# Operand tiles in slots of 4608 bytes with other row starts, in one step of a hybrid decoder on one core

## The chip, the cores and the metric

The kernel runs on one core of a Trainium2 chip. The metric is the device time of one execution in microseconds. Three runs of the kernel before took 1588.73, 1588.81 and 1589.09 us, a median of 1588.81.

## What is computed

One inference step of one decoder layer over 264 tokens: 8 sample tokens and a prompt of 256, each of 2048 features. The reference, cut to its order:

```python
proj = rmsnorm(x) @ w_in                       # 2048 x 6144: u_A, v_A, q, k, v, g
out_a = gelu(u) * chunk_spatial_mix(layernorm(gelu(v_A)))
out_b = silu(g) * groupnorm(retention(rotary(q), rotary(k), v, state))
h = x + concat(out_a, out_b) @ w_out           # 2048 x 2048
mk, mv = rmsnorm(mem) @ w_ck, rmsnorm(mem) @ w_cv      # 256 memory tokens
h = h + cross_attend(rmsnorm(h) @ w_cq, mk, mv) @ w_co # samples: cached keys, values
h = h + square(relu(rmsnorm(h) @ w_ff1)) @ w_ff2       # 2048 x 8192 x 2048
y = rmsnorm(h)
```

All data is float32. Outputs beside y are the memory's keys and values, the retention states and the normed rows of the sample tokens.

## The kernel before

Activations lie transposed: a feature block of 128 on the partitions, the 264 tokens along the free dimension. A tile of weights ("chunk" in the code) is 2 feature blocks of 128 by 512 output columns. Its float32 numbers are split into a rounded part and the rest, `wh` (cast by ScalarE, line 1064) and `wl` (subtracted by VectorE, line 1072). The activations are split in the same way into `xh` and `xl`, or under the names `h1`, `h2`, `mg`, `mu`, `o`, `q` and `r` with h and l behind. `group_act` (lines 156 to 158) issues per weight tile, for each of 4 column blocks m and each of the 2 feature blocks k, three matmuls: `wh` by `xh`, `wh` by `xl`, `wl` by `xh`. The weights stand still in the array and a row of activations, 264 numbers or 1056 bytes a partition, moves past them. That is 6 matmuls for each m and 24 for each tile.

Tiles of 264 columns: 12 column groups by 8 tiles of the input projection, 4 by 8 each of `w_out`, `w_cq` and `w_co`, 16 by 8 of `w_ff1` and 8 by 4 by 4 of `w_ff2`, whose very last group goes through `group_last` with the m outermost. The two projections of the memory tokens have operands of their own (`memh`, `meml`: rows of 256 numbers). `w_ck` goes through `group_act` with n=256, `w_cv` through `group_mem`, where the weights move.

A pair of operand tiles comes from `rows` (line 50): each holds four feature blocks, so `opnd_of` takes block kt from row kt % 4 of tile kt // 4, and the weight tiles of a group go through the rows 0, 1, then 2, 3, then 0, 1 of the next operand tile, and so on. `rows` takes one of 26 slots under the tag "s", which `slot` hands out for other things too. A slot is as large as its largest tile: here 4 rows by 272 numbers by 4 bytes, 4352 bytes, 17 times 256. In the built program the first slot begins at byte 72128 of a partition, which is 192 behind a multiple of 256. The rows are 1088 bytes apart, so the four rows of every tile begin 192, 0, 64 and 128 bytes behind a multiple of 256.

The order of the work is written out by hand. A loop over all 512 weight tiles issues the casts two or three tiles ahead, the loads up to six ahead (all on SP's queue), and the matmuls. After every 6 matmuls (fewer in some groups) `run_point` lets one deferred piece of other work go ahead: evictions, rotary, retention by head in two lanes, sample attention, stores. A store goes out ten such points after it was asked for. Retention of a head (line 601) copies the new prompt state out of PSUM into `so` (line 640), asks for its store, then scales the old state (line 642) and updates it by rows. Sample attention multiplies each loaded tile of cached keys or values with a broadcast query or probability on VectorE (lines 854 and 877). The sums are what is wanted; the products go to a scratch tile `jk` of the tag "hf".

Of the kernel before, what the change touches and what calls it, by code (L numbers as in the profile page):

```python
# [6 lines left out]
F32 = mybir.dt.float32  # L7
F32R = mybir.dt.float32r
AF = mybir.ActivationFunctionType
ALU = mybir.AluOpType  # L10
# [32 lines left out]
def _emit(tc, cst, wpool, spool, tpool, psum, dpool, I, O):  # L43
# [4 lines left out]
        return spool.tile(shape, dt, name=name, tag="s", bufs=NSLOT)  # L48

    def rows(name):  # L50
        return spool.tile([128, 4, 272], F32R, name=name, tag="s", bufs=NSLOT)

    def t264(name="t"):
        return tpool.tile([128, T], F32, name=name, tag="t", bufs=9)
# [5 lines left out]
        return tpool.tile([128, n], F32, name=name, tag="sm", bufs=24)  # L60

    def half(name, dt=F32):
        return tpool.tile([128, 512], dt, name=name, tag="hf", bufs=3)

    def bank(shape, name):
        return psum.tile(shape, F32, name=name, tag="mm", bufs=5)
# [228 lines left out]
            S[key] = r  # L295

    def opnd_of(tiles):
        return lambda kt: (tiles[kt // 4][0][:, kt % 4, 0:T], tiles[kt // 4][1][:, kt % 4, 0:T])

    def opnd_mem(kt):  # L300
        return tuple(t[:, kt % 4, :] for t in memop[kt // 4])
# [26 lines left out]

    def prep_x(s, ks=R4):
        for k in ks:  # L330
            split(A[s][0][:, k, 0:T], A[s][1][:, k, 0:T], hT[s][:, k, :], gain(G_N1, 4 * s + k))

    def square_x():
        q = []
# [73 lines left out]
    def ev_vA(g):  # L408
        def ev(ps):
            z = normed(ps)  # L410
            ge = slot([128, 4, T], "ge")
            if g == 0:
                sgu_loads()
                S["vn"] = [slot([128, 1024], "vn0"), slot([128, 1024], "vn1"), slot([8, 1024], "vns")]
                S["vsum"] = [small(2, "vsum") for _ in range(3)]

            def natural():
                for i, (c0, n) in enumerate(TOK):
                    tp = misc([n, 512], "tp")
                    for m in R4:  # L420
                        transpose(tp[:, m * 128:(m + 1) * 128], ge[:, m, c0:c0 + n])
                    act.activation(S["vn"][i][:, g * 512:(g + 1) * 512], tp[:], AF.Copy, scale=0.5,
                                   accum_out=S["vsum"][i][0:n, g:g + 1])
                    yield

            def gen():
                yield from gelu2(z, lambda m: ge[:, m, :])
                defer(natural(), 1)
                if g == 0:
                    chain(masks(), 12)  # L430
                else:
                    chain(layernorm(), 12)
                    for h in range(8):
                        defer(spatial(h), 56)
            chain(gen())
        return ev
# [26 lines left out]
    def masks():  # L463
        gp.tensor_tensor(out=S["wst"][:], in0=S["wst"][:], in1=trilt.unsqueeze(1).broadcast_to([128, 8, 128]),
                         op=ALU.mult)
        dg = cst.tile([8, 8, 8], F32, name="dg")
        gp.tensor_tensor(out=dg[:], in0=ident[0:8, 0:8].unsqueeze(1).broadcast_to([8, 8, 8]),
                         in1=w00[:].unsqueeze(2).broadcast_to([8, 8, 8]), op=ALU.mult)
        S["dg"] = dg
        yield  # L470
        S["spat"] = [slot([128, 4, T], "spat") for _ in range(2)]
# [19 lines left out]

    def split4(dst, src):
        for m in R4:
            act.copy(dst[0][:, m, 0:T], src[m][:])
        yield
        for m in R4:
            dve.tensor_tensor(out=dst[1][:, m, 0:T], in0=src[m][:], in1=dst[0][:, m, 0:T].bitcast(F32),
                              op=ALU.subtract)

    def pair(name):  # L500
# [76 lines left out]
    def sample_rows(g):  # L577
        if g == 0:
            S["kqd"], S["kqe"] = {}, {}
        cols = S["rpool"].tile([128, 2, 32], F32, name="kqcol", tag="kqcol", bufs=1)  # L580
        for i, w in enumerate("kq"):
            act.copy(cols[:, i, :].rearrange("p (m b) -> p m b", m=4), S[w][g][:, :, 0:8])
        yield 2
        tp = misc([32, 2, 128], "tp")
        for i in range(2):
            transpose(tp[:, i, :], cols[:, i, :])
        rows = half("kqrow")[0:32, 0:256]
        act.copy(rows, tp[:].rearrange("p a d -> p (a d)"))
        S["kqd"][g] = dpool.tile([32, 256], F32, name=f"kqd{g}")
        S["kqe"][g] = store(S["kqd"][g][:], rows, 3)  # L590
        yield
# [8 lines left out]
    def retention(h):  # L600
# [1 line left out]
        qt, kt, vt = S["q"][g][:, m, :], S["k"][g][:, m, :], S["v"][g][:, m, :]  # L602
        st, dec = S["state"].pop(h)

        def row(name):
            return S["rpool"].tile([128, 384], F32, name=name, tag="st", bufs=4)

        while g not in S["kqe"] or not S["kqe"][g][3]:
            yield 2
        yield 2  # L610
        ahead = rows_of(h, 0)
        kn, vn = row("kn"), row("vn")
        sm = S["rpool"].tile([128, 384], F32, name="sm", tag="sm", bufs=2)
        tp = misc([128, 256], "tp")
        for i in range(2):
# [20 lines left out]
        for i in range(2):  # L636
            c = slice(i * 128, (i + 1) * 128)
            pe.matmul(pp[:], lhsT=kn[:, c], rhs=vn[:, c], start=(i == 0), stop=(i == 1))
        so = S["rpool"].tile([128, 128], F32, name="so", tag="so", bufs=2)
        act.copy(so[:], pp[:])  # L640
        store(O["state_p"][h], so[:])
        act.activation(st[:], st[:], AF.Copy, scale=GAMMA[h])
# [72 lines left out]
    def ev_res(g, dst, st, gbase, name):  # L715
        def ev(ps):
            if g == 0:
                S[st] = Stats()
            dst.append(pair(name))
            oh, ol = dst[-1]  # L720
            h = [hT[g][:, m, :] for m in R4]
            for m in R4:
                dve.tensor_tensor(out=h[m], in0=h[m], in1=ps[m][:], op=ALU.add)

            def gen():
                for m in R4:
                    act.activation(oh[:, m, 0:T], h[m], AF.Copy, scale=gain(gbase, g * 4 + m))
                yield 2
                for m in R4:
                    dve.scalar_tensor_tensor(out=ol[:, m, 0:T], in0=h[m], scalar=gain(gbase, g * 4 + m),  # L730
                                             in1=oh[:, m, 0:T].bitcast(F32), op0=ALU.mult, op1=ALU.subtract)
                t = [S[st].square(h[m]) for m in R4]
                yield
                for m in R4:
                    S[st].add(t[m])
                if g == 3:
                    defer(S[st].finish(st + "r"), 8, front=True)
            chain(gen())
        return ev
# [48 lines left out]
    def ev_cq(h):  # L788
        def ev(ps):
# [16 lines left out]
            def gen():  # L806
                for m in R4:
                    act.copy(small8[:, m, :], z[m][:, 0:8])
                    act.copy(qh[:, m, 0:T], z[m][:])
                yield 4  # L810
                for m in R4:
                    gp.tensor_tensor(out=ql[:, m, 0:T], in0=z[m][:], in1=qh[:, m, 0:T].bitcast(F32), op=ALU.subtract)
            chain(gen())
            defer(sample_attn(h), 4, lane="kv")
        return ev
# [1 line left out]
    def join_o(h):  # L817
        if h in oT and h in oS:
            oh, ol = oT[h]
            split(oh[:, :, 0:8], ol[:, :, 0:8], oS[h][:])  # L820

    def softmax(s, n, then=None):
        mx, nb, sm, rc = small(1, "mx"), small(1, "nb"), small(1, "sm"), small(1, "rc")
# [14 lines left out]
    def sample_attn(h):  # L838
# [8 lines left out]
        for b in range(8):  # L847
            kv_fill()
            kc = kvq.popleft()
            qb = misc([128, 512], "qb")  # L850
            pe.matmul(qb[:], lhsT=sel[:, b:b + 1].broadcast_to([128, 128]), rhs=qs[:], start=True, stop=True)  # L851
            for i in range(2):
                jk = half("kjk")
                dve.scalar_tensor_tensor(out=jk[:], in0=kc[:, i * 512:(i + 1) * 512], scalar=1.0, in1=qb[:],
                                         op0=ALU.mult, op1=ALU.mult, accum_out=sc[:, i * 8 + b:i * 8 + b + 1])
            yield 5
            kv_fill()
# [12 lines left out]
        for b in range(8):  # L870
# [2 lines left out]
            pb = misc([128, 256], "pb")  # L873
            pe.matmul(pb[:], lhsT=sel[:, b:b + 1].broadcast_to([128, 128]), rhs=pst[:], start=True, stop=True)
            for d in R4:
                jk = half("vjk")
                dve.scalar_tensor_tensor(out=jk[:, 0:256], in0=vc[:, d * 256:(d + 1) * 256], scalar=1.0, in1=pb[:],
                                         op0=ALU.mult, op1=ALU.mult, accum_out=so[:, d, b:b + 1])
            yield 4
            kv_fill()  # L880
# [38 lines left out]
    def prompt_attn(h, mk, vh, vl):  # L919
# [2 lines left out]
        ps = []  # L922
        for tq in range(2):
            sc = misc([128, 256], "sc")
            c = slice(8 + tq * 128, 136 + tq * 128)
            for k in R4:
                pe.matmul(sc[:], lhsT=qh[:, k, c], rhs=kh[:, k, :], start=(k == 0), stop=False)
                pe.matmul(sc[:], lhsT=qh[:, k, c], rhs=kl[:, k, :], start=False, stop=False)
                pe.matmul(sc[:], lhsT=ql[:, k, c], rhs=kh[:, k, :], start=False, stop=(k == 3))
            ps.append(softmax(sc[:], 128))  # L930
            yield 6 if tq else 2
        tp = misc([128, 2, 256], "tp")
# [13 lines left out]
        for d in R4:  # L946
            op = misc([128, 256], "op")
            for mt in range(2):
# [1 line left out]
                pe.matmul(op[:], lhsT=a, rhs=ph[mt][:, 0:256], start=(mt == 0), stop=False)  # L950
                pe.matmul(op[:], lhsT=a, rhs=pl[mt][:, 0:256], start=False, stop=False)
                pe.matmul(op[:], lhsT=b, rhs=ph[mt][:, 0:256], start=False, stop=(mt == 1))
            split(oh[:, d, 8:T], ol[:, d, 8:T], op[:])
            yield 2


# [2 lines left out]
    def ev_ff1(b, g):  # L959
        def ev(ps):  # L960
# [6 lines left out]

            def gen():
                for m in R4:
                    act.activation(rh[:, m, 0:T], r[m][:], AF.Square)  # L970
                    act.activation(r[m][:], r[m][:], AF.Square)
                yield 4
                for m in R4:
                    dve.tensor_tensor(out=rl[:, m, 0:T], in0=r[m][:], in1=rh[:, m, 0:T].bitcast(F32), op=ALU.subtract)
            chain(gen())
        return ev

# [265 lines left out]
```

## Time and profile before

| | |
|---|---|
| median of three runs | 1588.81 us |
| the profiled execution | 1588.74 us |
| its span | 1587.0 us |
| VectorE busy | 1038.5 us, 65% |
| ScalarE busy | 748.3 us, 47% |
| GpSimd busy | 122.0 us, 8% |
| read from memory, written | 321.42 MB, 11.17 MB: 210 GB/s |

Busy times are those of each engine's instructions within the span. Durations of matmuls overlap, since one flows into the array behind the other. The timeline gives the start and the duration of each instruction, in microseconds from the start of the span. In the list of waits a row names the engine and line that waited, whom it waited for, the total in us, how often, and the longest.

### The profile page before, as it was taken

How to read it: one execution, taken by the hardware profiler on the slowest of the kernel's cores; microseconds unless marked ns; L12 is line 12 of the kernel's file. 1: busy time of each engine (PE TensorE's matmuls, PEld its weight loads, DVE VectorE, ACT ScalarE, POOL GpSimd, SP SyncE). 2: the span in 40 equal slices, each digit the busy share in tenths (PEclk: the TensorE clock that was granted, in tenths of full speed). 3: DMA queues.
4: the chain of work that ended last, by engine and by line, in shares of the span. 5: the costliest groups of instructions: out<-in, count | busy, mean ns of one | idle time of the engine just before them, and what ended most of it. 6: DMA issues, size and time to landing. Idle time of an engine off the chain costs nothing.

```text
span 1587.0 us, 30814 instructions
## 1 busy us (share of the span) xinstructions
PE 1573.1 (99%) x12515; PEld 1546.7 (97%) x12515; DVE 1038.5 (65%) x1875; ACT 748.3 (47%) x1165; POOL 122.0 (8%) x111
## 2 busy tenths in 40 slices
PE   9999999999999999999999999999999999999997
PEld 8999999999999998899999999999999999999997
DVE  6677798778677777876665555555555565555555
ACT  7445566357544444444454543434344353444443
POOL 0332122110011201010000000000000000000000
PEclk9999999999999999999999999999999999999999
DMA  8587876456578878976555555565555555555552
GB/s 290 189 268 258 288 242 195 159 188 226 179 261 318 299 275 290 318 246 244 183 175 186 175 183 174 184 187 170 188 184 175 185 173 188 175 185 186 170 183 89
DMA packets 98927, 334.61 MB, mean 211 GB/s; under 512 B 11152, under 2 KB 16336, under 8 KB 98784
## 3 DMA queue, kind: packets, MB, share of 16 engines
q1 hardware_dynamic: 98784, 332.64, 63.1%
q8 instruction: 98, 1.61, 0.4%
q14 instruction: 45, 0.37, 0.1%
HBM read 321.42 MB, written 11.17 MB: 210 GB/s over the span
## 4 chain that ended last, share of the span: by engine, by line
PE 49%; issue 47%; DVE 2%; DMA 1%; POOL 0%; SPq 0%; DVEq 0%; ACT 0%; POOLq 0%
PE acc L156 13%; PE acc L158 13%; PE acc L157 13%; PE acc L180 2%; PE acc L182 2%; PE acc L181 2%; PE tp L100 1%; DVE wl L1072 1%; DMA bkq<-kqd 1%; PE qb L851 0%; DMA w<-in_w_in_dram 0%; DVE state L651 0%; PE spp L479 0%; DVE bkq L653 0%; PE op L950 0%
## 5 line engine op out<-in xcount | busy, mean ns | idle before, releaser
L1064 ACT CAST wh<-w 128x1024 fp32r<-128x1024 f32 (+1 forms) x513 | 535.8, 1045 | 696.9 <-PE acc L157 620.4
L1072 DVE TENSOR_TENSOR wl<-w,wh 128x1024 fp32r<-128x1024 f32 (+1 forms) x513 | 626.4, 1233 | 261.9 <-ACT wh L1064 259.0
L156 PE MATMUL acc<-h2h,wh 128*128 128x264 f32 x1024 | 291.4, 285 | 0.0
L158 PE MATMUL acc<-h2h,wl 128*128 128x264 f32 x1024 | 291.1, 284 | 0.0
L157 PE MATMUL acc<-h2l,wh 128*128 128x264 f32 x1024 | 290.5, 284 | 0.0
L156 PE MATMUL acc<-rh,wh 128*128 128x264 f32 x992 | 282.2, 284 | 0.0
L158 PE MATMUL acc<-rh,wl 128*128 128x264 f32 x992 | 282.0, 284 | 0.0
L157 PE MATMUL acc<-rl,wh 128*128 128x264 f32 x992 | 281.4, 284 | 0.0
L156 PE MATMUL acc<-xh,wh 128*128 128x264 f32 x768 | 224.8, 293 | 2.4 <-DVE vt L557 1.2
L158 PE MATMUL acc<-xh,wl 128*128 128x264 f32 x768 | 218.7, 285 | 0.4 <-DVE wl L1092 0.2
L157 PE MATMUL acc<-xl,wh 128*128 128x264 f32 x768 | 217.5, 283 | 0.1
L157 PEld LDWEIGHTS acc<-h2l,wh 128*128 128x128 f32 x1024 | 192.8, 188 | 0.0
L156 PEld LDWEIGHTS acc<-h2h,wh 128*128 128x128 f32 x1024 | 192.6, 188 | 0.0
L158 PEld LDWEIGHTS acc<-h2h,wl 128*128 128x128 f32 x1024 | 192.4, 188 | 0.0
L157 PEld LDWEIGHTS acc<-rl,wh 128*128 128x128 f32 x992 | 186.8, 188 | 0.0
L156 PEld LDWEIGHTS acc<-rh,wh 128*128 128x128 f32 x992 | 186.6, 188 | 0.0
L158 PEld LDWEIGHTS acc<-rh,wl 128*128 128x128 f32 x992 | 186.4, 188 | 0.0
L156 PEld LDWEIGHTS acc<-xh,wh 128*128 128x128 f32 x768 | 144.7, 188 | 4.3 <-DVE vt L557 1.4
L157 PEld LDWEIGHTS acc<-xl,wh 128*128 128x128 f32 x768 | 144.9, 189 | 0.3 <-DVE xl L108 0.3
L158 PEld LDWEIGHTS acc<-xh,wl 128*128 128x128 f32 x768 | 144.3, 188 | 0.9 <-DVE wl L1092 0.4
L982 DVE TENSOR_TENSOR hT<-hT,acc 128x264 f32<-128x264 f32 x124 | 53.2, 429 | 73.2 <-PE acc L158 73.2
L96 POOL TENSOR_TENSOR msr<-msv,neghalf 128x3 f32<-128x3 f32 (+1 forms) x5 | 7.8, 1560 | 983.6 <-DVE msv L272 737.6
(249 smaller groups left out, 2745.3 us busy)
## 6 DMA issues: line engine op xcount, KB each, us to landing
w<-in_w_ff_dram SPq DMA_DIRECT2D x256, 512.0 KB, 3.8
w<-in_w_in_dram SPq DMA_DIRECT2D x95, 512.0 KB, 4.1
w<-in_w_out_dram SPq DMA_DIRECT2D x32, 512.0 KB, 3.7
w<-in_w_cq_dram SPq DMA_DIRECT2D x32, 512.0 KB, 4.3
kv<-in_kN_dram SPq DMA_DIRECT2D x32, 512.0 KB, 5.5
kv<-in_vT_dram SPq DMA_DIRECT2D x32, 512.0 KB, 5.1
w<-in_w_ck_dram SPq DMA_DIRECT2D x32, 512.0 KB, 5.4
w<-in_w_cv_dram SPq DMA_DIRECT2D x32, 512.0 KB, 4.6
```

The source lines that it names most:

```text
L96: gp.tensor_tensor(out=out, in0=in_, in1=neghalf[0:in_.shape[0], 0:n], op=ALU.pow)
L100: pe.transpose(out, in_, ident[0:p, 0:p])
L156: pe.matmul(ps, lhsT=a, rhs=xh, start=(i == 0), stop=False)
L157: pe.matmul(ps, lhsT=a, rhs=xl, start=False, stop=False)
L158: pe.matmul(ps, lhsT=b, rhs=xh, start=False, stop=(i == nk - 1))
L180: pe.matmul(ps, lhsT=a, rhs=hi[:, k, :], start=(kt == 0), stop=False)
L181: pe.matmul(ps, lhsT=a, rhs=lo[:, k, :], start=False, stop=False)
L182: pe.matmul(ps, lhsT=b, rhs=hi[:, k, :], start=False, stop=(kt == 15))
L982: dve.tensor_tensor(out=h[m], in0=h[m], in1=ps[m][:], op=ALU.add)
L1064: act.copy(hi[:, k, :], raws[i][:, k, :])
L1072: dve.tensor_tensor(out=lo[:, k, :], in0=raw[:, k, :], in1=hi[:, k, :].bitcast(F32), op=ALU.subtract)
```

## The change

`rows` now makes a tile of 2 pairs by 576 numbers, 4608 bytes or 18 times 256. The second row of a pair still begins 1088 bytes behind the first, and the second pair begins 2304 bytes (9 times 256) behind the first pair. `row` gives the part of a tile that was `[:, k, c0:c1]`, and `heads` the first n columns of all four rows. The first slot now begins at byte 71872, again 192 behind a multiple of 256, since the constants lost the 256 bytes of `dg`. So the rows of every operand tile begin 192, 0, 192 and 0 bytes behind a multiple of 256. All other tiles of slots begin 192 behind one, as before.

The slots need 26 by 256 = 6656 bytes more. They come from `dg` (now the end of the slot tile `vns`), from two of the three "hf" buffers (products of sample attention are written over the keys or values that they read), and from the retention's pool: `kqcol` goes to the shared "t" buffers, `kn` and `vn` have tags of their own with 256 numbers instead of 384 for `vn`, and `so` has one buffer instead of two.

```diff
     def rows(name):
-        return spool.tile([128, 4, 272], F32R, name=name, tag="s", bufs=NSLOT)
+        return spool.tile([128, 2, 576], F32R, name=name, tag="s", bufs=NSLOT)
+
+    def row(t, k, c0=0, c1=T):
+        b = 272 * (k % 2)
+        return t[:, k // 2, b + c0:b + c1]
+
+    def heads(t, n):
+        return t[:, :, 0:544].rearrange("p a (b f) -> p a b f", b=2)[:, :, :, 0:n]
...
-        return tpool.tile([128, 512], dt, name=name, tag="hf", bufs=3)
+        return tpool.tile([128, 512], dt, name=name, tag="hf", bufs=1)
...
     def opnd_of(tiles):
-        return lambda kt: (tiles[kt // 4][0][:, kt % 4, 0:T], tiles[kt // 4][1][:, kt % 4, 0:T])
+        return lambda kt: (row(tiles[kt // 4][0], kt % 4), row(tiles[kt // 4][1], kt % 4))
...
-                S["vn"] = [slot([128, 1024], "vn0"), slot([128, 1024], "vn1"), slot([8, 1024], "vns")]
+                S["vn"] = [slot([128, 1024], "vn0"), slot([128, 1024], "vn1"), None]
+                S["vns"] = slot([8, 1088], "vns")
+                S["vn"][2] = S["vns"][:, 0:1024]
...
-        dg = cst.tile([8, 8, 8], F32, name="dg")
+        dg = S["vns"][:, 1024:1088].rearrange("p (h b) -> p h b", h=8)
...
-        cols = S["rpool"].tile([128, 2, 32], F32, name="kqcol", tag="kqcol", bufs=1)
+        cols = t264("kqcol")[:, 0:64].rearrange("p (i c) -> p i c", i=2)
...
-        kn, vn = row("kn"), row("vn")
+        kn = S["rpool"].tile([128, 384], F32, name="kn", tag="kn", bufs=2)
+        vn = S["rpool"].tile([128, 256], F32, name="vn", tag="vn", bufs=2)
...
-        so = S["rpool"].tile([128, 128], F32, name="so", tag="so", bufs=2)
+        so = S["rpool"].tile([128, 128], F32, name="so", tag="so", bufs=1)
...
-            split(oh[:, :, 0:8], ol[:, :, 0:8], oS[h][:])
+            split(heads(oh, 8), heads(ol, 8), oS[h][:].rearrange("p (a b) f -> p a b f", a=2))
...
-                jk = half("kjk")
-                dve.scalar_tensor_tensor(out=jk[:], in0=kc[:, i * 512:(i + 1) * 512], scalar=1.0, in1=qb[:],
+                ki = kc[:, i * 512:(i + 1) * 512]
+                dve.scalar_tensor_tensor(out=ki, in0=ki, scalar=1.0, in1=qb[:],
...
-                jk = half("vjk")
-                dve.scalar_tensor_tensor(out=jk[:, 0:256], in0=vc[:, d * 256:(d + 1) * 256], scalar=1.0, in1=pb[:],
+                vd = vc[:, d * 256:(d + 1) * 256]
+                dve.scalar_tensor_tensor(out=vd, in0=vd, scalar=1.0, in1=pb[:],
```

The other lines of the diff write the same ranges through `row`. On every engine the instructions stand in the same order as before, and so do the loads and stores on SP's queue; what differs is some waits. On ScalarE, at the fourth head's copy into `so`, the built program had before, with what each row waits for:

```order
L588 COPY kqrow<-tp 32x256 [waits PE_49]
L640 COPY so<-pp 128x128 [waits DMAHW6_49,PE_49]
L642 ACTIVATE state<-state 128x1024
L1064 CAST wh<-w 128x1024 [waits DMAHW2_49,Activation_49]
L1064 CAST wh<-w 128x1024 [waits DMAHW4_49,DVE_49,PE_49]
```

And at the same place it now has:

```order
L597 COPY kqrow<-tp 32x256 [waits DMAHW1_49,PE_49]
L647 COPY so<-pp 128x128 [waits DMAHW2_49,PE_49,Activation_49]
L649 ACTIVATE state<-state 128x1024
L1071 CAST wh<-w 128x1024
L1071 CAST wh<-w 128x1024 [waits DMAHW4_49,DVE_49,PE_49]
```

No row moved. The store that the copy waits for was that of two heads before; it is now that of the head before.

More of the change, by code (lines that the diff above doesn't have):

```diff
@@ L330, in prep_x @@
         for k in ks:
-            split(A[s][0][:, k, 0:T], A[s][1][:, k, 0:T], hT[s][:, k, :], gain(G_N1, 4 * s + k))
+            split(row(A[s][0], k), row(A[s][1], k), hT[s][:, k, :], gain(G_N1, 4 * s + k))
     def square_x():
@@ L465, in masks @@
                          op=ALU.mult)
-        dg = cst.tile([8, 8, 8], F32, name="dg")
-        gp.tensor_tensor(out=dg[:], in0=ident[0:8, 0:8].unsqueeze(1).broadcast_to([8, 8, 8]),
+        dg = S["vns"][:, 1024:1088].rearrange("p (h b) -> p h b", h=8)
+        gp.tensor_tensor(out=dg, in0=ident[0:8, 0:8].unsqueeze(1).broadcast_to([8, 8, 8]),
                          in1=w00[:].unsqueeze(2).broadcast_to([8, 8, 8]), op=ALU.mult)
@@ L493, in split4 @@
         for m in R4:
-            act.copy(dst[0][:, m, 0:T], src[m][:])
+            act.copy(row(dst[0], m), src[m][:])
         yield
         for m in R4:
-            dve.tensor_tensor(out=dst[1][:, m, 0:T], in0=src[m][:], in1=dst[0][:, m, 0:T].bitcast(F32),
+            dve.tensor_tensor(out=row(dst[1], m), in0=src[m][:], in1=row(dst[0], m).bitcast(F32),
                               op=ALU.subtract)
@@ L603, in retention @@
         st, dec = S["state"].pop(h)
-        def row(name):
-            return S["rpool"].tile([128, 384], F32, name=name, tag="st", bufs=4)
         while g not in S["kqe"] or not S["kqe"][g][3]:
@@ L726, in gen @@
                 for m in R4:
-                    act.activation(oh[:, m, 0:T], h[m], AF.Copy, scale=gain(gbase, g * 4 + m))
+                    act.activation(row(oh, m), h[m], AF.Copy, scale=gain(gbase, g * 4 + m))
                 yield 2
                 for m in R4:
-                    dve.scalar_tensor_tensor(out=ol[:, m, 0:T], in0=h[m], scalar=gain(gbase, g * 4 + m),
-                                             in1=oh[:, m, 0:T].bitcast(F32), op0=ALU.mult, op1=ALU.subtract)
+                    dve.scalar_tensor_tensor(out=row(ol, m), in0=h[m], scalar=gain(gbase, g * 4 + m),
+                                             in1=row(oh, m).bitcast(F32), op0=ALU.mult, op1=ALU.subtract)
                 t = [S[st].square(h[m]) for m in R4]
@@ L808, in gen @@
                     act.copy(small8[:, m, :], z[m][:, 0:8])
-                    act.copy(qh[:, m, 0:T], z[m][:])
+                    act.copy(row(qh, m), z[m][:])
                 yield 4
                 for m in R4:
-                    gp.tensor_tensor(out=ql[:, m, 0:T], in0=z[m][:], in1=qh[:, m, 0:T].bitcast(F32), op=ALU.subtract)
+                    gp.tensor_tensor(out=row(ql, m), in0=z[m][:], in1=row(qh, m).bitcast(F32), op=ALU.subtract)
             chain(gen())
@@ L924, in prompt_attn @@
             sc = misc([128, 256], "sc")
-            c = slice(8 + tq * 128, 136 + tq * 128)
+            c0 = 8 + tq * 128
             for k in R4:
-                pe.matmul(sc[:], lhsT=qh[:, k, c], rhs=kh[:, k, :], start=(k == 0), stop=False)
-                pe.matmul(sc[:], lhsT=qh[:, k, c], rhs=kl[:, k, :], start=False, stop=False)
-                pe.matmul(sc[:], lhsT=ql[:, k, c], rhs=kh[:, k, :], start=False, stop=(k == 3))
+                pe.matmul(sc[:], lhsT=row(qh, k, c0, c0 + 128), rhs=kh[:, k, :], start=(k == 0), stop=False)
+                pe.matmul(sc[:], lhsT=row(qh, k, c0, c0 + 128), rhs=kl[:, k, :], start=False, stop=False)
+                pe.matmul(sc[:], lhsT=row(ql, k, c0, c0 + 128), rhs=kh[:, k, :], start=False, stop=(k == 3))
             ps.append(softmax(sc[:], 128))
@@ L952, in prompt_attn @@
                 pe.matmul(op[:], lhsT=b, rhs=ph[mt][:, 0:256], start=False, stop=(mt == 1))
-            split(oh[:, d, 8:T], ol[:, d, 8:T], op[:])
+            split(row(oh, d, 8), row(ol, d, 8), op[:])
             yield 2
@@ L969, in gen @@
                 for m in R4:
-                    act.activation(rh[:, m, 0:T], r[m][:], AF.Square)
+                    act.activation(row(rh, m), r[m][:], AF.Square)
                     act.activation(r[m][:], r[m][:], AF.Square)
@@ L973, in gen @@
                 for m in R4:
-                    dve.tensor_tensor(out=rl[:, m, 0:T], in0=r[m][:], in1=rh[:, m, 0:T].bitcast(F32), op=ALU.subtract)
+                    dve.tensor_tensor(out=row(rl, m), in0=r[m][:], in1=row(rh, m).bitcast(F32), op=ALU.subtract)
             chain(gen())
```

## The prediction

> **What bounds the kernel now.** I read the page first, for the busiest engine and its clock, then the groups of section 5 for who waits for whom, then the timeline of TensorE alone, matmul by matmul.
>
> ```profile
> PE 1573.1 (99%) x12515; PEld 1546.7 (97%) x12515; DVE 1038.5 (65%) x1875; ACT 748.3 (47%) x1165; POOL 122.0 (8%) x111
> PEclk9999999999999999999999999999999999999999
> L1064 ACT CAST wh<-w 128x1024 fp32r<-128x1024 f32 (+1 forms) x513 | 535.8, 1045 | 696.9 <-PE acc L157 620.4
> L1072 DVE TENSOR_TENSOR wl<-w,wh 128x1024 fp32r<-128x1024 f32 (+1 forms) x513 | 626.4, 1233 | 261.9 <-ACT wh L1064 259.0
> ```
>
> TensorE is busy for 99% of the span at the full granted clock. ScalarE, which casts the weights, spends 620.4 us waiting for TensorE to give its buffers back, so the weights are ahead of the matmuls and not behind them. Only the rate at which matmuls start can move the end. A busy matmul overlaps its neighbours (about 0.28 us each below, while one starts every 0.12 us), so the rate has to be read from starts. Here is the beginning of one pass of 16 weight tiles of 24 matmuls each (start, duration). Of every six matmuls, those of one column block m over the tile's two rows, only the first is shown.
>
> ```profile
> 966.88 0.29 PE L156 MATMUL acc<-h2h,wh 128*128 128x264 f32 x1
> 967.61 0.28 PE L156 MATMUL acc<-h2h,wh 128*128 128x264 f32 x1
> 968.34 0.28 PE L156 MATMUL acc<-h2h,wh 128*128 128x264 f32 x1
> ...
> 969.78 0.28 PE L156 MATMUL acc<-h2h,wh 128*128 128x264 f32 x1
> 970.51 0.28 PE L156 MATMUL acc<-h2h,wh 128*128 128x264 f32 x1
> 971.24 0.28 PE L156 MATMUL acc<-h2h,wh 128*128 128x264 f32 x1
> 971.97 0.29 PE L156 MATMUL acc<-h2h,wh 128*128 128x264 f32 x1
> 972.72 0.29 PE L156 MATMUL acc<-h2h,wh 128*128 128x264 f32 x1
> ...
> 974.17 0.28 PE L156 MATMUL acc<-h2h,wh 128*128 128x264 f32 x1
> ...
> 975.62 0.28 PE L156 MATMUL acc<-h2h,wh 128*128 128x264 f32 x1
> ...
> 980.00 0.28 PE L156 MATMUL acc<-h2h,wh 128*128 128x264 f32 x1
> ...
> 981.45 0.28 PE L156 MATMUL acc<-h2h,wh 128*128 128x264 f32 x1
> ```
>
> The first tile (966.88 to 969.78) reads operand rows that begin 192 and 0 bytes behind a multiple of 256; call it an even tile. It takes 2.90 us, in sixes of 0.73, 0.73 and then 1.44 for the last two. The second (to 972.72) reads rows that begin 64 and 128 bytes behind one, an odd tile. It takes 2.94 us, in sixes of 0.73, 0.73, 0.73 and 0.75. The third, even again, takes 2.90 (to 975.62). Even and odd tiles alternate through the whole pass:
>
> ```profile
> 966.88:1013.55 46.67, 46.67 (x387) 46.67 (x385) 24.16 (x28) 19.66 (x24) 0.00 (x0) 1.00 0.57 181
> 1013.55:1060.21 46.66, 46.66 (x386) 46.66 (x385) 27.21 (x36) 19.67 (x24) 0.00 (x0) 1.00 0.59 180
> ```
>
> A pass of eight pairs lasts 46.67 us, and the next one, with another operand in other slots, 46.66. So a pair of tiles costs 46.67 / 8 = 5.834 us: 2.90 for the even tile and 2.93 for the odd one, or 0.729 a six.
>
> Does the row's start do this, or something else that alternates from tile to tile, such as the weight buffer? The projection of the memory tokens tells them apart. Its rows are 1024 bytes long and always begin 192 bytes behind a multiple of 256, while its weight tiles come from the same alternating buffers:
>
> ```profile
> 590.13 0.28 PE L156 MATMUL acc<-memh,wh 128*128 128x256 f32 x1
> ...
> 593.01 0.39 PE L851 MATMUL qb<-qs,sel 128*128 128x512 f32 x1
> 593.24 0.28 PE L156 MATMUL acc<-memh,wh 128*128 128x256 f32 x1
> ...
> 596.12 0.40 PE L180 MATMUL acc<-wh,memh 128*128 128x512 f32 x1
> ```
>
> Two neighbouring tiles take 593.01 - 590.13 = 2.88 and 596.12 - 593.24 = 2.88 us, 0.72 a six. With the start held, nothing alternates. That puts the difference on the moving operand's start.
>
> **The change part by part.**
>
> *Rows.* The slots grow from 17 to 18 times 256 bytes and the second pair of rows moves to 2304 bytes, 9 times 256. Every tile of 264 columns becomes an even tile. By the code these are 96 tiles of the input projection, 32 each of the output, query and attention-output projections, and 128 each of the two MLP layers: 448 tiles, 224 pairs. What does an even tile cost when the tile ahead of it is even too? No stretch of this trace has that, but the four sixes of an even tile show the direction: they start at 0.73, right behind an odd tile, and their last two take 969.78 - 968.34 = 1.44, 975.62 - 974.17 = 1.45 and 981.45 - 980.00 = 1.45 us, a mean of 0.7233 each. The odd tile goes the other way, from 0.73 to 0.75. So a six seems to depend on its own rows and on what ran before, and I take the late value as the one that stays: eight sixes by 0.7233 = 5.787 us a pair, 0.047 less than now, and 224 by 0.047 = **10.5 us** less. From below the gain is bounded by the even tile as it stands (2.90 for both tiles: 5.834 - 5.80 = 0.034, by 224 = 7.6 us), from above by the memory tiles' 0.72 (5.834 - 5.76 = 0.074, by 224 = 16.6 us). Where other matmuls stand between the sixes, in the input projection above all, I take the same gain.
>
> A rule of the Trainium skill speaks against any gain: "SBUF — State Buffer", section "Specifications (TRN2)", gives lines of 16 bytes, with a penalty for each cross to a new line. All row starts, old and new, are multiples of 64, so every row has the same 66 lines, and by that rule the change would be worth nothing. The sixes of 0.73 and 0.75 at one clock and one shape disagree with it; I go by the rows.
>
> *One `so` buffer instead of two.* The copy of a head's state now waits on ScalarE until the store of the head before has landed, and behind it stand the scaling of the state and the weight casts. Below are the copies and the stores ahead of them from the timelines, the stores' time to landing, and two rows of the waits from 95 to 260 us.
>
> ```profile
> 110.09 0.27 ACT L640 COPY so<-pp 128x128 f32<-128x128 f32 x1 [1.63 <-PE pp L638]
> 149.99 0.27 ACT L640 COPY so<-pp 128x128 f32<-128x128 f32 x1 [2.66 <-PE pp L638]
> 190.92 0.27 ACT L640 COPY so<-pp 128x128 f32<-128x128 f32 x1 [0.35 <-PE pp L638]
> 107.44 0.43 SPq L231 DMA_DIRECT2D out_state_p_dram<-so  x1
> 148.37 0.43 SPq L231 DMA_DIRECT2D out_state_p_dram<-so  x1
> 188.36 0.34 SPq L231 DMA_DIRECT2D out_state_p_dram<-so  x1
> DMA to landing us min/median/max: 3.5/4.1/5.4
> ACT wh L1064 <- PE acc L157: 10.1, 10, 1.9
> DVE wl L1072 <- ACT wh L1064: 2.1, 3, 0.8
> ```
>
> With the median of 4.1 us these stores land at 111.5, 152.5 and 192.5, so three copies wait 1.5, 2.5 and 1.5 us, 5.5 in all. I cost them at nothing: the last two rows show ScalarE waiting for TensorE ten times and VectorE waiting for a cast for 2.1 us only, so the casts lead by more than a stall. If that cover were gone, TensorE would pay up to 5.5 us; none of it can be a gain.
>
> *In-place products, other scratch.* The products against the cached keys and values now overwrite the tile that they read. For the same shape, an in-place result costs what another costs:
>
> ```profile
> L982 DVE TENSOR_TENSOR hT<-hT,acc 128x264 f32<-128x264 f32 x124 | 53.2, 429 | 73.2 <-PE acc L158 73.2
> L389 DVE TENSOR_TENSOR z<-acc,rstd 128x264 f32<-128x264 f32 x24 | 9.9, 428 | 7.2 <-PE acc L158 7.2
> ```
>
> 429 against 428 ns, and VectorE has a third of the span to spare. The next load into such a tile waited for the same product before. The key and query columns in the shared scratch, the narrower rows of keys and values, the spatial table in a slot and the finer view of the joined heads change neither the count nor the sizes of any work. Zero, and hidden by the same idle time of both engines.
>
> *Sum.* The profiled execution took 1588.74 us, 1.74 outside its span of 1587.0; 1588.74 - 10.5 = 1578.2. The median of the three runs is 0.07 above the profiled one: **1578.3 us**.
>
> **The rivals.**
> - *The tile before does not matter.* Every tile costs what an even one costs now, 2.90: a gain of 7.6 us, 1581.2. For it speaks that its price is measured as it stands; against it, that equal rows give 0.73 and later 0.72 inside one tile.
> - *All the way down.* A longer run of equal starts settles at the memory tiles' 0.72: a gain of 16.6 us, 1572.2. For it: those tiles have equal starts. Against it: their rows are 32 bytes shorter and all begin at 192.
> - *The start does nothing.* The odd tiles' extra time comes from their place and stays: 1588.8. The line rule of "SBUF — State Buffer" in the Trainium skill would give this. Against it: the two memory tiles of 2.88.
> - *The drift goes on.* The sixes of a tile move with what ran before. If a run of even tiles longer than four sixes climbs, as the odd tile does, to the mean of that tile's last two sixes, (972.72 - 971.24) / 2 = 0.74, a pair costs 5.92, 0.086 more than now, by 224 = 19.3 us: 1608.1, slower. It decides from a mean six above 0.729. Against it: the even tile's sixes fall, and never rise.
>
> **How the numbers follow.** Forecast 0.47, the even tile as it stands 0.25, all the way down 0.12, nothing 0.10, the drift 0.06. What a measurement can tell from no change is about 0.2%, 3.2 us. The first three lie beyond it: faster 0.84, same 0.10, slower 0.06. The range takes those three and reaches from 1572 to 1585; the top is the 1581.2 of the first rival and most of the 5.5 us of uncovered `so` waits.
>
> **What would show it.** In TensorE's timeline a pass of 16 tiles should last 64 by 0.7233 = 46.3 us in place of 46.67, with odd and even tiles alike. A pass of 46.4 is the first rival, one of 46.1 the second, one of 46.67 the third. If the passes are shorter and the total isn't, the time went into the first 320 us, and the `so` copies, now released by the store's landing, and casts behind them would show it. The forecast is wrong if equal tiles do not get equal times.

## The result, and the profile after

The changed kernel takes 1579.29 us, the median of six runs (1578.35 to 1581.44), against 1588.92 for the kernel before in six runs: a ratio of 0.994, with a 95% interval of 0.9927 to 0.9953. That is 9.6 us less; 10.5 were forecast. The profiled execution is the slowest of the six (1581.44, span 1579.6), so its rows carry some 2 us more than the median; where they lie is shown below.

The page of the changed kernel: the share of TensorE, its clock, and the waiting of the casts. Lines have moved by 7 (L163 to L165 are the old L156 to L158).

```profile
PE 1563.9 (99%) x12515; PEld 1537.5 (97%) x12515; DVE 1037.8 (66%) x1875; ACT 747.9 (47%) x1165; POOL 122.4 (8%) x111
PEclk9999999999999999999999999999999999999999
L1071 ACT CAST wh<-w 128x1024 fp32r<-128x1024 f32 (+1 forms) x513 | 536.0, 1046 | 683.4 <-PE acc L164 596.6
```

TensorE is still 99% busy, at the full clock as far as slices of 39 us show it, and ScalarE still waits for it. What has changed above all is the pace. TensorE's timeline of the same pass of 16 tiles, the first of every six matmuls:

```profile
964.33 0.28 PE L163 MATMUL acc<-h2h,wh 128*128 128x264 f32 x1
...
965.05 0.28 PE L163 MATMUL acc<-h2h,wh 128*128 128x264 f32 x1
...
965.77 0.28 PE L163 MATMUL acc<-h2h,wh 128*128 128x264 f32 x1
...
966.50 0.28 PE L163 MATMUL acc<-h2h,wh 128*128 128x264 f32 x1
...
967.22 0.28 PE L163 MATMUL acc<-h2h,wh 128*128 128x264 f32 x1
...
967.94 0.28 PE L163 MATMUL acc<-h2h,wh 128*128 128x264 f32 x1
...
968.67 0.28 PE L163 MATMUL acc<-h2h,wh 128*128 128x264 f32 x1
...
969.39 0.28 PE L163 MATMUL acc<-h2h,wh 128*128 128x264 f32 x1
...
970.11 0.28 PE L163 MATMUL acc<-h2h,wh 128*128 128x264 f32 x1
```

Eight sixes in 970.11 - 964.33 = 5.78 us. None of them stands out: the 0.73 at a tile's beginning is gone, and so are the odd tile's 0.74 and 0.75. The whole pass and the next, in the view of busy time by stretch (start and end, length, then each engine's busy time and count):

```profile
964.33:1010.62 46.29, 46.29 (x386) 46.29 (x385) 24.16 (x28) 19.68 (x24) 0.00 (x0) 1.00 0.57 184
1010.62:1056.91 46.29, 46.29 (x386) 46.29 (x385) 27.30 (x36) 19.68 (x24) 0.00 (x0) 1.00 0.57 182
```

46.29 / 64 = 0.7233 a six. The 448 tiles are 28 such passes; if all gained as much, 28 by (46.67 - 46.29) = 10.6 us came from the pace. That is an estimate from one pass. The first 16 tiles of the output projection, for one, took 46.67 us before (325.65 to 372.32) and now run at 46.08 / 64 = 0.720 a six:

```profile
326.77:372.85 46.08, 46.08 (x386) 46.08 (x385) 37.83 (x63) 30.50 (x56) 4.00 (x4) 1.00 0.67 221
```

Part of it was given back between 95 and 260 us. There, the waits of TensorE before the change and VectorE's for the state, and after it the same with those of ScalarE's `so` copy for a store (total us, times, longest):

```profile
DVE state L651 <- ACT state L642: 1.9, 3, 1.4
PE acc L156 <- DVE vt L557: 1.2, 1, 1.2
PE rp L100 <- DVE bkq L653: 0.3, 1, 0.3
```

```profile
PE acc L163 <- DVE vt L566: 1.9, 1, 1.9
PE acc L163 <- DVE ra L538: 0.8, 1, 0.8
PE rp L107 <- DVE bkq L660: 0.7, 1, 0.7
ACT so L647 <- DMA out_state_p_dram<-so: 12.3, 3, 5.8
DVE state L658 <- ACT state L649: 5.9, 7, 2.1
```

TensorE waited 1.5 us in this stretch before and 3.4 after. None of it is for a cast. It waits for VectorE, to free an accumulator (`ra`, `vt`) or to finish a row of the state (`bkq`). VectorE in turn waits for the state that ScalarE scales behind the held-up copy: 5.9 us against 1.9 before. ScalarE's copy shows the three waits for a store that were forecast, but longer.

The wait for `vt` had a second price in this execution. TensorE starts nothing from 159.82 to 161.96 us, and behind that its matmuls start every 0.22 us instead of every 0.12. The granted clock is the third figure from the end of each line:

```profile
162.00:164.00 2.00, 2.00 (x10) 2.00 (x11) 2.00 (x4) 1.36 (x7) 0.00 (x0) 0.53 0.81 249
164.00:166.00 2.00, 2.00 (x12) 2.00 (x12) 1.90 (x9) 0.14 (x1) 0.40 (x1) 0.61 0.43 115
```

It is 0.53 and 0.61 there and 1.00 in the stretches before and behind; over a slice of 39 us it still rounds to a 9. In the profile before, the same wait lasted from 159.98 to 161.50 and the clock stayed at 1.00.

### The profile page after: what moved, and what is told of

Same layout as the page of the kernel before. It is cut to its first block, busy times and chain, and to the rows that moved or that the text cites. A ratio compares the mean times of both kernels' runs of the same rounds, so it can differ in the third digit from the quotient of the medians.

```text
span 1579.6 us, 30820 instructions
## 1 busy us (share of the span) xinstructions
PE 1563.9 (99%) x12515; PEld 1537.5 (97%) x12515; DVE 1037.8 (66%) x1875; ACT 747.9 (47%) x1165; POOL 122.4 (8%) x111
## 4 chain that ended last, share of the span: by engine, by line
issue 47%; PE 47%; DVE 2%; DMA 2%; ACT 0%; SPq 0%; POOL 0%; DVEq 0%; ACTq 0%; POOLq 0%
PE acc L163 13%; PE acc L165 13%; PE acc L164 12%; PE acc L187 2%; PE acc L189 2%; PE acc L188 2%; DMA out_state_p_dram<-so 1%; DVE wl L1079 1%; DMA w<-in_w_in_dram 1%; PE tp L107 1%; PE qb L858 0%; DVE state L658 0%; DVE bkq L660 0%; PE spp L488 0%; DMA bkq<-kqd 0%
## 5 line engine op out<-in xcount | busy, mean ns | idle before, releaser
L165 PE MATMUL acc<-h2h,wl 128*128 128x264 f32 x1024 | 290.9, 284 | 0.0
L163 PE MATMUL acc<-h2h,wh 128*128 128x264 f32 x1024 | 290.6, 284 | 0.0
L165 PE MATMUL acc<-rh,wl 128*128 128x264 f32 x992 | 281.8, 284 | 0.0
L163 PE MATMUL acc<-rh,wh 128*128 128x264 f32 x992 | 281.3, 284 | 0.0
L163 PE MATMUL acc<-xh,wh 128*128 128x264 f32 x768 | 224.9, 293 | 3.9 <-DVE vt L566 1.9
L165 PE MATMUL acc<-xh,wl 128*128 128x264 f32 x768 | 218.8, 285 | 0.4 <-DVE wl L1079 0.2
L165 PEld LDWEIGHTS acc<-h2h,wl 128*128 128x128 f32 x1024 | 192.5, 188 | 0.0
L163 PEld LDWEIGHTS acc<-h2h,wh 128*128 128x128 f32 x1024 | 192.3, 188 | 0.0
L165 PEld LDWEIGHTS acc<-rh,wl 128*128 128x128 f32 x992 | 186.5, 188 | 0.0
L163 PEld LDWEIGHTS acc<-rh,wh 128*128 128x128 f32 x992 | 186.3, 188 | 0.0
L163 PEld LDWEIGHTS acc<-xh,wh 128*128 128x128 f32 x768 | 145.3, 189 | 5.9 <-DVE vt L566 2.1
L165 PEld LDWEIGHTS acc<-xh,wl 128*128 128x128 f32 x768 | 145.0, 189 | 0.9 <-DVE wl L1099 0.4
```

Source lines behind the costliest of these rows:

```text
L163: pe.matmul(ps, lhsT=a, rhs=xh, start=(i == 0), stop=False)
L165: pe.matmul(ps, lhsT=b, rhs=xh, start=False, stop=(i == nk - 1))
```

## The experiments

Times are medians. Runs of one group share a chip and the kernel before, whose median there was 1588.3 to 1588.6.

**Only the row starts undone.** Slots of 4608 bytes and all other edits stay; the four rows are 1088 bytes apart again.

```diff
-        return spool.tile([128, 2, 576], F32R, name=name, tag="s", bufs=NSLOT)
+        return spool.tile([128, 1152], F32R, name=name, tag="s", bufs=NSLOT)
...
-        b = 272 * (k % 2)
-        return t[:, k // 2, b + c0:b + c1]
+        b = 272 * k
+        return t[:, b + c0:b + c1]
...
```

> The changed kernel with its slots of 4608 bytes and all its smaller scratch, but the four rows of a tile 1088 bytes apart as before, so that they begin 192, 0, 64 and 128 bytes behind a multiple of 256. Theory, that the row starts alone make the gain: the sixes go back to 0.73, 0.73, 0.72, 0.72 and 0.73, 0.72, 0.74, 0.74, a pass of 16 tiles to 46.67 us, the time to 1579.3 + 10.9 = 1590.2. Rival, that the larger slots or the other scratch made it: 1579.3.

1589.65 us, a ratio of 1.0008 (0.9999 to 1.0017). The pass is back to the hundredth:

```profile
967.76:1014.43 46.67, 46.67 (x386) 46.67 (x385) 24.16 (x28) 19.62 (x24) 0.00 (x0) 1.00 0.56 182
```

The row starts make the gain. The 1 us above the kernel before looks like a cost of the rest; the next two runs look for it.

**Two `so` buffers again**, with the new row starts and with the old ones.

```diff
-        so = S["rpool"].tile([128, 128], F32, name="so", tag="so", bufs=1)
+        so = S["rpool"].tile([128, 128], F32, name="so", tag="so", bufs=2)
...
```

> The changed kernel with two so buffers again (the room comes from a smaller scratch tile; one cast of zeros is made in two halves). Theory, that the stalls of the so copies reach TensorE: the three waits for a store on ScalarE (12.3 us in the changed kernel's profile) go, the three gaps of TensorE at 131, 160 and 200 us fall from 1.07, 2.14 and 0.97 us back to about 0.40, 1.52 and 0.59, so 1.7 us less: about 1577.6. Rival, that they are hidden as forecast: 1579.3, no change.

> The changed kernel with the old row starts (192, 0, 64, 128) and two so buffers: what is left of the change is its larger slots, its in-place products and its other scratch. Theory, that row starts and so buffers are all that counts: 1588.6, the time of the kernel before, 1.1 less than with the old starts and one buffer (1589.65). Rival, that one of the other edits costs or gains: it stays at 1589.6 or falls below 1588.

With the new starts 1578.31 us, a ratio of 0.9935 (0.9918 to 0.9952); with the old ones 1588.33, a ratio of 0.9999 (0.999 to 1.0008). Against the runs with one buffer that is 1.0 and 1.3 us less, where 1.7 and 1.1 were expected. TensorE's waits from 95 to 260 us with two buffers and the new starts:

```profile
PE acc L163 <- DVE vt L566: 0.9, 1, 0.9
PE rp L107 <- DVE bkq L660: 0.4, 1, 0.4
PE acc L163 <- DVE ra L538: 0.3, 1, 0.3
```

1.6 us in all, about the 1.5 of the kernel before. So one `so` buffer costs about 1 us by these pairs. It is no fixed price: the run with everything moved, below, has one buffer too and took 1578.57, 0.3 above the run with two on the same chip. With it undone and the old starts, the time is that of the kernel before: the larger slots, the in-place products and the other scratch cost nothing that can be measured. Each difference of 1 us is smaller than the intervals of its two runs; that both pairs show it, and that the waits go with it, is what carries it. The profiled executions say the same: the first tile of the output projection starts at 323.49 us with two buffers, and with one buffer at 326.77 in the execution above, at 324.87 in the next run and at 324.45 in the one with everything moved.

**The changed kernel once more.**

> The changed kernel once more, unchanged, on the same chip as the next run and the runs of before. 1579.3; both theories of the so copies agree here, and it gives the spread that its store waits bring: the kernel before has spread by 1 us, this one by 3.

1579.18 us (1578.73 to 1580.93), a ratio of 0.9943 (0.9931 to 0.9956). Its spread is 2.2 us, that of the run with two buffers 0.6. Its profiled execution (1579.45) has 3.4 us of the same waits of TensorE as the one shown above, but the wait for `vt` is 0.4 us shorter and the clock stays at 1.00 behind it; the output projection starts 1.9 us earlier. So the half clock behind the wait is most of what the profiled execution of the changed kernel lost against the median. The run with starts 0 and 64, whose profiled execution is again its slowest, shows the same (a clock of 0.50 from 166 to 168 us). What decides whether the clock drops is not shown.

**Other pairs of row starts.** The rows move up within their slots by 128 or by 64 bytes (`heads` with them); nothing else changes. The diff shows 128 bytes, 32 numbers; for 64 bytes it is 16. The weights stay 192 behind a multiple of 256.

```diff
-        b = 272 * (k % 2)
+        b = 32 + 272 * (k % 2)
...
```

> The changed kernel with all rows moved up by 128 bytes within their slots: every pair begins 64 and 128 bytes behind a multiple of 256. Theory, that a pair of starts has a rate of its own which a run of equal tiles settles at: the last sixes of the odd tiles before (0.74 us) everywhere, 1792 sixes by 0.74 - 0.723 = 30 us more than the changed kernel, about 1610. First rival, that a tile costs what it cost before whatever ran ahead of it: the odd tiles' 2.93 us everywhere, 0.7325 a six, 17 us more, about 1596. Second rival, that only the alternation between the two kinds of pairs costs, and any equal pair is as fast as any other: 1579.3.

> The changed kernel with all rows moved up by 64 bytes within their slots: pairs begin 0 and 64 bytes behind a multiple of 256, while the weights stay 192 behind one. The run with everything moved by 64 had the same starts and kept sixes of 0.723 us. Theory, that only the distance from weights to rows counts (0 and 64 in the changed kernel, here 64 and 128): the sixes leave 0.723; with one row of the good pair and one of the bad one (128 and 192, 0.740) about 0.731, so 1792 by 0.008 = 14 us more, about 1593, anywhere from 1579 to 1610. Rival, that the starts 0 and 64 are good by themselves: 0.723 and 1579.3.

Starts 64 and 128: 1606.41 us, a ratio of 1.0111 (1.0096 to 1.0126). Starts 0 and 64: 1590.84, a ratio of 1.0019 (1.001 to 1.0028). Their passes, the first line of each:

```profile
976.18:1023.54 47.36, 47.36 (x387) 47.36 (x385) 24.16 (x28) 19.66 (x24) 0.00 (x0) 1.00 0.55 179
```

```profile
972.35:1019.00 46.65, 46.65 (x387) 46.65 (x385) 24.16 (x28) 19.67 (x24) 0.00 (x0) 1.00 0.54 182
```

47.36 / 64 = 0.740 a six for 64 and 128, and 0.729 for 0 and 64. The first shows what a run of equal tiles does in these passes. It goes to the rate of the odd tile's last sixes, (0.73 + 0.75) / 2, and not to that tile's mean. (Not everywhere: 13 tiles of the input projection, from 50.19 to 88.32 us, run at 0.733.) The rival by which alternation alone costs is out: this pair is equal everywhere and the slowest of all.

**Weights and rows moved together, and a fourth pair.** 64 more bytes of constants move everything; 192 unused bytes between weights and slots (with two `so` buffers) move only the slots.

```diff
+    cst.tile([128, 16], F32, name="shift")
```

```diff
+    wpool.tile([128, 48], F32, name="space", tag="space", bufs=1)
```

> The changed kernel with 64 more bytes of constants, which move the weight tiles, the slots and all behind them up by 64: weights and operand tiles begin at a multiple of 256 instead of 192 behind one, rows 0 and 64 behind. If what counts is where the moving rows begin relative to the weights, nothing changes: 1579.3 and sixes of 0.723. If it is where the moving rows begin by themselves, the pair 0, 64 has another rate, not seen so far, up to the 0.74 of the odd tiles' last sixes: up to 30 us more, 1610. The memory tiles, then beginning at 0, would leave their 0.72 too.

> The changed kernel with two so buffers and 192 unused bytes between the weight tiles and the slots, so that rows begin 128 and 192 bytes behind a multiple of 256 and the weights still 192: distances 192 and 0, the fourth pair of neighbours. All other tiles in slots move with them, the memory tokens' too (distance 192 instead of 0). Theory of the distance: neither the 0.723 of the pair 0 and 64 nor the 0.740 of 128 and 192; between them, about 0.731 and 1592. Rival, that the absolute starts 128 and 192 count: not seen together so far, so any rate; the pair 64 and 128 at the same weights had 0.740. If it beats 0.723 it is the better kernel: at 0.720 it would take 1573.

Everything moved: 1578.57 us, a ratio of 0.9935 (0.992 to 0.995). The slots alone moved: 1591.94, a ratio of 1.0023 (1.0014 to 1.0032). Their passes:

```profile
961.89:1008.19 46.30, 46.30 (x387) 46.30 (x385) 24.16 (x28) 19.68 (x24) 0.00 (x0) 1.00 0.56 183
```

```profile
966.71:1013.64 46.93, 46.93 (x386) 46.93 (x385) 24.17 (x28) 19.63 (x24) 0.00 (x0) 1.00 0.54 181
```

Rows at 0 and 64 with weights at 0 keep the good 46.30; the same rows with weights at 192 take 46.65. So the row's address by itself does not set the rate. Its distance from the weights fits in the two cases where one can be held against the other; but the run with everything moved shifts all that lies behind the constants, so it does not single out the weights. The memory tokens' tiles, now at 0 with weights at 0, keep their 2.88 us (590.05 to 592.93). By distance the four neighbouring pairs stand so in these passes: 0 and 64 at 0.723 a six, 64 and 128 at 0.729, 192 and 0 at 0.733, 128 and 192 at 0.740.

**One distance for every matmul.** If the pair were a mean of two distances, one of them held constant should be better still. These kernels start from the kernel before (slots of 4352 bytes, rows 1088 apart) and pad the cast weight tiles so that their halves and buffers step as the rows do; unused bytes behind them set the distance: 48 numbers for 192 as shown, 16 for 64, 32 for 128 and none for 0. They also have two "hf" buffers, and the memory tokens' rows are 1088 bytes apart in them too.

```diff
+    def cast_tile(name):
+        return wpool.tile([128, 2, 528], F32R, name=name, tag=name, bufs=N_CAST)[:, :, 0:512]
...
+    wpool.tile([128, 48], F32, name="space", tag="space", bufs=1)
```

> The kernel before (old slots of 4352 bytes, rows 1088 bytes apart, scratch as before but two hf buffers), with the cast weight tiles padded so that they step like the rows: the second half of a tile begins 64 bytes later within 256 than the first, the next buffer 128 later. Every matmul with weights standing then has the same distance from its weights to its row, here 192, by 192 unused bytes ahead of the slots. Theory, that the distance in steps of 64 sets the rate, and that the memory tokens' matmuls at distance 192 (0.680 to 0.707 us a six, against 0.720 at distance 0) show what a constant 192 gives: 0.70 a six with 32 bytes more, 1792 by 0.729 - 0.70 = 52 us less than the kernel before, about 1537. Rival, that rows of 1056 bytes are not helped, or that alternation within the tile matters and not the distance: between 0.720 and 0.733 a six, 1573 to 1596.

> The same with 64 unused bytes, a constant distance of 64. In pairs the distances 0 and 64 had 0.723 a six, 64 and 128 had 0.729, 128 and 192 had 0.740, 192 and 0 had 0.733. If a pair is the mean of its two distances, 64 is as good as 0 and both are better than 192, which contradicts the expectation of the run above: about 0.72 and 1573. If the change of distance from row to row costs, every constant distance beats its pairs: below 0.72, 1570 or less. If neither, 1580 to 1590.

> The padded weight tiles without unused bytes: a constant distance of 0 from weights to rows. The constant distances 192 and 64 gave 0.734 and 0.733 a six, no better than the pairs. The memory tokens' rows, at distance 0 with weights that do not step, gave 0.720. If distance 0 is the good one, 0.720 to 0.723: 1573 to 1578. If stepping the weights themselves costs, as the two constant distances suggest, 0.730 or more: 1590 or later.

> The same with a constant distance of 128. If stepping weights cost about 0.733 at any distance: 1592 to 1596 as at 64 and 192. If the distance still counts and 128 is the bad one of the slow pair (128 and 192 gave 0.740): above 0.740, 1605 or more.

| distance | median, us | ratio to before | pass, us | a six |
|---|---|---|---|---|
| 192 | 1595.96 | 1.0046 (1.0029 to 1.0063) | 46.99 | 0.734 |
| 64 | 1592.67 | 1.0027 (1.0017 to 1.0037) | 46.98 | 0.734 |
| 128 | 1596.25 | 1.0049 (1.0032 to 1.0066) | 46.98 | 0.734 |
| 0 | 1587.4 | 0.9995 (0.9986 to 1.0004) | 46.82 | 0.732 |

No theory is met. At 192 and 128 the rivals come close: 0.734 a six where up to 0.733 was given, 1595.96 and 1596.25 us where up to 1596 was. At 64 and 0 the times miss the rivals' ranges too, by 2.7 and 2.6 us. In these passes no constant distance comes near the 0.723 of the changed kernel, and distances of 64, 128 and 192 give the same pass. Here the weights step too, from one half tile to the next, which they did in no other run.

But one pass is not the kernel. At distance 0 the same addresses, shapes and clock show two rates. The output projection and most of `w_co` run at 0.721, the MLP passes at 0.732, one of each:

```profile
325.13:371.27 46.14, 46.14 (x387) 46.14 (x385) 37.84 (x63) 30.49 (x56) 4.00 (x4) 1.00 0.62 220
963.91:1010.73 46.82, 46.82 (x386) 46.82 (x385) 24.16 (x28) 19.64 (x24) 0.00 (x0) 1.00 0.55 181
```

The MLP's first three tiles run at 0.721 too. At 832.70 us the matmuls of a norm (`msq`, then `rsb`) stand between, and from there until the last group it is 0.731 to 0.732. So the distance from a matmul's own weights to its own row does not explain the rate by itself. What else does is open: the distance to the weights loaded next, or to the row before, would have to be varied one at a time, which these runs do not do, and what picks one of two rates would have to be found.

## Why the prediction was right, by its steps

- *TensorE's pace is the bound.* It held: the time followed the length of the pass in the runs that moved only rows, 46.29 at 1579, 46.65 at 1591 and 47.36 at 1606 us. The runs with padded weights do not follow it so closely (46.82 at 1587), since their other stages have other rates.
- *The row start makes the odd tiles slow.* That the starts are the lever is shown by undoing them alone: 46.67 and 1589.65. The prediction put the difference on the moving row's own start, and that is too narrow: rows at 0 and 64 run at 0.723 or 0.729, by where the weights lie. Its control, the memory tokens, could not tell, since weights and rows both begin at 192 there.
- *A run of even tiles settles at the tile's late value.* Forecast 0.7233 a six and 46.3 a pass; measured 0.7233 and 46.29. The first rival (each even tile at 2.90, 46.4) is out. The second (0.72, 46.1) is out for the MLP, but it is what most of the output projection does: of the 373 tiles with no other matmul among theirs, 35 run at 0.720 a six, and nearly all others at 0.723 to 0.724. By 4 sixes and 0.0033 that is 0.5 us, so the forecast's one late value is right for most of the kernel and not for all. The same reading put the run with starts 64 and 128 at about 1610, and it took 1606.41; the other reading had said 1596. That an even tile's sixes drift upward is out as well.
- *The start does nothing.* This rival, which the line rule of the Trainium skill ("SBUF — State Buffer", section "Specifications (TRN2)") would have given, falls with the runs: all starts are multiples of 64, and the pass went from 46.29 to 47.36.
- *The `so` copies cost nothing.* This term was mis-sized. It measured about 1 us (1.0 and 1.3 between medians, 0.3 in the run with everything moved), within the bound of 5.5 that was kept. Two things were wrong in it. The waits were longer: of the 12.3 us the same three copies had waited 1.63, 2.66 and 0.35 us for TensorE before, so 7.6 came on top and not 5.5, mostly because the stores took 4.2, 4.6 and 5.2 us to land in the profiled execution and not 4.1. And the cover was sought among the casts alone, which did hide it. The instructions that did not are VectorE's evictions and state updates, which stand in order behind the late state, and for which TensorE waits. That a longer wait can be followed by a stretch at half clock was not thought of at all.
- *The other scratch costs nothing.* Shown by the run with old starts and two `so` buffers, 1588.33 against 1588.36. The prediction took the price of an in-place product from other instructions; the products themselves took 683 and 416 ns each before (keys, values) and 683 and 415 in place.

Together: 10.6 us from the pace less 1.0 for the copies is 9.6, which is what the medians differ by. That this closes to a tenth is partly luck, since the first is one pass taken 28 times and the second a difference smaller than the intervals of its runs. Without the copies the gain was measured as 1588.58 - 1578.31 = 10.3 us. The 1578.3 of the forecast, which put the copies at nothing, is the time of that run with two `so` buffers, the fastest kernel here.

## What to carry to other kernels

Where matmuls run back to back and TensorE is the bound, read the starts of single matmuls over one period of the address pattern. A difference that repeats with the address is a price per matmul that no busy time shows, and a control with a fixed address in the same trace tells it from some of the other things that alternate, but not from those that hold still with it. Read the rate in more than one stage before it is taken for all. Behind a wait of TensorE, read the granted clock in stretches of 2 us and not by the page's slices. When memory is taken from a small tile to pay for it, count everything that stands in order behind the instruction that now waits, on the next engine too, and not only the work with the largest lead.

## What was not expected of the hardware

Memory tokens (rows of 1024 bytes, weights that do not step) at a distance of 192 ran well below the 0.72 us a six that had looked like a floor. In the run where the slots alone moved, one of their tiles begins and ends so in TensorE's timeline:

```profile
593.11 0.28 PE L163 MATMUL acc<-memh,wh 128*128 128x256 f32 x1
...
595.83 0.39 PE L187 MATMUL acc<-wh,memh 128*128 128x512 f32 x1
```

24 matmuls in 2.72 us, 0.68 a six or 113 ns each, against 2.88 at distance 0. It was not had for rows of 1056 bytes at any distance that was tried, nor for the memory tokens once weights and rows stepped: there their undisturbed tiles take 0.708 to 0.716 a six.

A repeating sequence of matmuls also settles in more than one rhythm. Sixes at starts 64 and 128 alternate between about 0.745 and 0.735 in the output projection and the MLP, and it takes a few sixes after a change of rows to get there. And one kernel can hold two rates with the same addresses. Counted from the starts of the 373 tiles of 264 columns that have no other matmul among theirs, left out those few around an interruption:

| run | us a six, tiles |
|---|---|
| changed kernel | 0.720 in 35, 0.722 to 0.725 in 324 |
| starts 64 and 128 | 0.733 to 0.735 in 20, 0.740 in 339 |
| starts 0 and 64 | 0.728 to 0.730 in 349, 0.740 in 12 |
| distance 0 | 0.719 to 0.721 in 79, 0.731 to 0.732 in 280 |
| distance 64 | 0.728 in 39, 0.730 to 0.731 in 27, 0.733 to 0.734 in 294 |

In the two cases followed here the rate changed where other matmuls stood between: at distance 0 at 832.70 us, in the changed kernel in the third column group of the output projection, at 390 us. Not every such interruption changes it. So the starts narrow down the rate, and what ran before seems to pick it; the mechanism under this is not settled by these runs.
